# Transposes in a one-core encoder step: issued in groups, or one by one between the projections' matmuls

## The chip, the cores and the metric

The kernel runs on one core of a Trainium2 chip. The metric is device time in microseconds (us) of one execution. TensorE (PE, with its weight loads as PEld), VectorE (DVE), ScalarE (ACT), GpSimd (POOL) and the DMA queues of SyncE (SP) work side by side, each through its own list of instructions, and wait for one another by semaphores.

## What is computed

One inference step of a streaming encoder: two layers over 512 rows of a prompt and 8 x 16 rows of running streams, 640 rows in all, width 1024. The rows go through the same weights. Each layer adds a normalised mixer and then a normalised gated feed-forward block to its rows:

```python
for layer in range(DEPTH):
    hp = rms_norm(xp, norm_mix_pre[layer])
    hs = rms_norm(xs, norm_mix_pre[layer])
    if layer % 2 == 0:     # gated spatial mixing and a short convolution
        mp, _, hist_p = even_mixer(hp, zero_hist, *prm)
        ms, vn_s, hist_s = even_mixer(hs, cache_conv[e], *prm)
    else:                  # pooling over trailing windows, and attention
        mp, np_p, k_p, v_p = odd_mixer(hp, zero_pool, pos_p, *prm, None, None)
        ms, np_s, k_s, v_s = odd_mixer(hs, cache_pool[o], pos_s, *prm, cache_k[o], cache_v[o])
    xp = xp + rms_norm(mp, norm_mix_post[layer])
    xs = xs + rms_norm(ms, norm_mix_post[layer])
    fp = swiglu(rms_norm(xp, norm_ffn_pre[layer]), ffn_w_gate[layer], ffn_w_up[layer], ffn_w_down[layer])
    fs = swiglu(rms_norm(xs, norm_ffn_pre[layer]), ffn_w_gate[layer], ffn_w_up[layer], ffn_w_down[layer])
    xp = xp + rms_norm(fp, norm_ffn_post[layer])
    xs = xs + rms_norm(fs, norm_ffn_post[layer])
```

A mixer is `h @ w_in`, its two halves side by side, and `@ w_out`. The attention of the odd mixer has 8 heads of 64; a prompt row sees its own and earlier rows, a stream's 16 rows see 512 cached rows and each other.

## The kernel before

The 640 rows are five row tiles of 128, t = 0 to 3 of the prompt and t = 4 of the streams. The program runs the even mixer, a feed-forward block, the odd mixer and a second feed-forward block. Products are in fp32 accuracy: each operand is split into a high and a low part in the fast 32-bit format, on ScalarE (the cast, high) and on VectorE (the subtraction, low), and a product is three matmuls, high by high, high by low and low by high. Most of the mixers' and gates' products go through a seven-product scheme over halves of 320 rows (`Seven`, `GateUp`, with the operand tiles of `Quarters`): those are the matmuls with 320 columns. The value projections (`v_proj`) and output projections (`out_chunk`) have matmuls with 512 columns.

A matmul contracts over partitions, so a row tile must be turned first. `pre_norm` (L352) normalises a row tile into `xn`, issues eight 128x128 transposes of it on TensorE (`flip`, L169) into two PSUM banks, and then has the bank pair split by `take` (L317) into the operand tiles. The four normalisations make 160 transposes. In attention `prompt_stream` (L1083) turns the probabilities of two heads per item (80 transposes in 16 items), and `sample_stream` (L1151) turns five tiles of probabilities and then one of outputs per item (48 in 8 items). ScalarE copies the turned probabilities out of PSUM, and the products with the values follow.

What stands where on TensorE is decided twice. `Weave` (L48) runs generators: `main` (priority 9) issues the projections and yields every 6 to 15 matmuls; `pre_norm` (priority 0) and the attention streams (priority 1) go ahead of it when they are due. Due times are on an estimated clock, `W.now`, that every matmul and every transpose moves on. The framework's scheduler then sets the final order on each engine by its own estimates, with the instructions of `tc.high_priority()` first; in the first mixer ScalarE's and VectorE's first instructions stay in program order (`Ordered`, L87, its helper line is L99).

Line numbers of the profile: matmuls are L167, transposes L171, ScalarE's and VectorE's instructions L99, the reciprocal root on GpSimd L234.

Of the kernel before, what the change touches and what calls it, by code (L numbers as in the profile page):

```python
# [1 line left out]

# [12 lines left out]
P = 128  # L15
# [32 lines left out]
class Weave:  # L48
# [6 lines left out]
    def __init__(self):  # L55
        self.now = 0.0
        self.tasks = []
        self.made = 0

    def spawn(self, gen, prio=0, wait=0.0):  # L60
        self.made += 1
# [3 lines left out]
        event.at = self.now + wait  # L65

    def run(self):
        def due(t):
            return t[2].at if isinstance(t[2], Event) else t[2]

        while self.tasks:
            known = [t for t in self.tasks if due(t) is not None]
            assert known, "every task waits"
            ready = [t for t in known if due(t) <= self.now]
            if not ready:
                self.now = min(due(t) for t in known)
                continue
            t = min(ready, key=lambda t: t[:2])
            try:
                r = next(t[3])  # L80
            except StopIteration:
                self.tasks.remove(t)
                continue
            t[2] = r if isinstance(r, Event) else self.now + (r or 0.0)
# [21 lines left out]
def trunk_kernel(  # L106
# [57 lines left out]
    def mm(out, lhsT, rhs, start, stop, n, share=1, more=False):  # L164
        fast = lhsT.dtype == F32R
        W.now += PASS * (max(n, 256) if fast else 4 * n / share) + 2
        nc.tensor.matmul(out, lhsT=lhsT, rhs=rhs, start=start, stop=stop, skip_group_check=more)  # L167

    def flip(out, in_):  # L169
        W.now += 109  # L170
        nc.tensor.transpose(out=out, in_=in_, identity=ident)  # L171

    uid = [0]

# [4 lines left out]
    def bank(shape=(P, 512)):  # L179
        return psp.tile(list(shape), F32, tag="ps", name=nm("ps"))  # L180
# [171 lines left out]
    def pre_norm(t, x, X, wait, xn=None):  # L352
        if xn is None:
            xn = t4([P, D])
        with tc.high_priority():
            norm = Norm()
            norm.add(x, xn)
            r = norm.get()
            dve.scalar_tensor_tensor(out=xn, in0=x, scalar=r, in1=X.gain, op0=ALU.mult, op1=ALU.mult)
        yield wait  # L360
        ps = []
        for half in range(2):
            ps.append(bank((P, HK, P)))
            for i in range(HK):
                k = HK * half + i
                flip(ps[half][:, i, :], xn[:, k * P : (k + 1) * P])
        yield 500
        X.take(t, ps)

    class PostNorm:  # L370
# [562 lines left out]
    def odd_mixer(X):  # L933
# [149 lines left out]
        def prompt_stream(items):  # L1083


            for j, qt in items:
# [22 lines left out]
                for pr, sm in prs:  # L1109
                    ri = st()  # L1110
                    dve.reciprocal(out=ri, in_=sm)
                    dve.tensor_scalar(out=pr[:, :n], in0=pr[:, :n], scalar1=ri, scalar2=None, op0=ALU.mult)
                yield 2200 + 5 * n
                for h in range(2):
                    s, pr = ss[h], prs[h][0]
                    for kt in range(qt + 1):
                        flip(s[:, kt * P : (kt + 1) * P], pr[:, kt * P : (kt + 1) * P])
                    act.copy(out=pr[:, :n], in_=s[:, :n])
                yield 600 + 1.5 * n
                if j not in pos:  # L1120
                    pos[j] = bank()
                po = pos[j]
# [28 lines left out]
        def sample_stream(items):  # L1151
            for b in items:
# [31 lines left out]
                dve.tensor_tensor(out=ri, in0=sm[:, 0:1], in1=sm[:, 1:2], op=ALU.add)  # L1184
                dve.reciprocal(out=ri, in_=ri)
                yield 3300
                for kt in range(5):
                    flip(s[:, kt * P : (kt + 1) * P] if kt < 4 else s2[:, :P], pr[:, kt, :])
                pt = t2([P, 5, P])
                act.copy(out=pt[:, 0:4, :].rearrange("p a c -> p (a c)"), in_=s)  # L1190
                dve.tensor_copy(out=pt[:, 4, :], in_=s2[:, :P])
# [16 lines left out]
                os_ = pt[:, 0, :]  # L1208
                dve.tensor_scalar(out=os_, in0=o, scalar1=ri, scalar2=None, op0=ALU.mult)
                yield 500  # L1210
                flip(s2[:, 2 * P : 3 * P], os_)
                ot = s2[:, 2 * P : 3 * P].rearrange("p (a c s) -> p a c s", a=4, c=2)
                for h in range(2):
                    r = slice(64 * h, 64 * h + 64)
# [49 lines left out]
    def main():  # L1264
# [20 lines left out]
        next(first)  # L1285
        hls = [operand(w[0])]
        for _ in first:
            pass
        W.signal(X.top[0])
        hls.append(operand(w[1]))  # L1290
        start(1, A1)
# [118 lines left out]
```

## Time and profile before

| | us |
|---|---|
| median of three timed runs | 1320.55 (1320.53 to 1320.88) |
| the profiled execution | 1320.24 |
| its span | 1318.5 |
| TensorE busy | 1294.0 (98%) |
| VectorE busy | 889.0 (67%) |
| ScalarE busy | 614.0 (47%) |
| transposes, records of all 288 | 42.2 |

The span is the time from the profile's first to its last record. Busy shares are of that span. A record's length is the time from its issue to its modelled end, and records of neighbours overlap on TensorE, so the sum of records of a group is more than the time it takes on the array. Names of tiles in the rows are cut to their stem; `ps` is a PSUM bank, `q` the split of a weight, `x` and `a` splits of rows, `t` other tiles, `st` statistics.

### The profile page before, as it was taken

Reading aid. Unit: us, or ns where it says so; the run is one execution under the profiler, and the core shown is the slowest. Engines: PE = TensorE matmul, PEld = TensorE weight load, DVE = VectorE, ACT = ScalarE, POOL = GpSimd, SP = SyncE. Lnnn points to the kernel's source line nnn. Section 1 sums busy time; section 2 is a strip of 40 time slices with the busy share of each in tenths; the row PEclk is TensorE's granted clock in tenths of the full one; section 3 lists DMA queues with packets and bytes.
Section 4 is the critical chain, followed back from the end, with each engine's and each line's share of the span. In section 5 each row is a group of like instructions: output and inputs, shape, how many; then the busy total and the mean of one; then the engine's idle time right before and its main releaser. Section 6 shows DMA issues by size and latency. Waiting matters only on the chain.

```text
span 1318.5 us, 20069 instructions
## 1 busy us (share of the span) xinstructions
PE 1294.0 (98%) x8060; PEld 1178.4 (89%) x8060; DVE 889.0 (67%) x1452; ACT 614.0 (47%) x1130; POOL 54.9 (4%) x107
## 2 busy tenths in 40 slices
PE   6999999999999999999999999999999999999997
PEld 5998989989899998998799885789999898998996
DVE  6985779837576675776736556489557575864766
ACT  5644546535254352454433455366455261551551
POOL 2200101000000000000210000010000000000000
PEclk9999999999999999999999999999999999999999
DMA  7212253212223122126435336532213021230233
GB/s 249 73 65 81 96 200 138 96 48 81 96 73 120 53 77 112 64 84 218 163 120 195 147 143 250 197 128 102 107 64 128 32 98 63 96 115 30 97 128 128
DMA packets 45965, 150.12 MB, mean 114 GB/s; under 512 B 6576, under 2 KB 8496, under 8 KB 45872
## 3 DMA queue, kind: packets, MB, share of 16 engines
q1 hardware_dynamic: 45872, 148.84, 31.2%
q8 instruction: 63, 1.03, 0.3%
q14 instruction: 30, 0.25, 0.1%
HBM read 133.57 MB, written 15.26 MB: 113 GB/s over the span
## 4 chain that ended last, share of the span: by engine, by line
PE 86%; DVE 5%; issue 3%; ACT 2%; DMA 2%; POOL 1%; SPq 0%; DVEq 0%; POOLq 0%; ACTq 0%
PE ps L167 84%; DVE t L99 3%; PE ps L171 1%; DMA xbuf<-t 1%; POOL st L234 1%; ACT t L99 1%; DMA raw<-in_dram 1%; DVE q L99 1%; ACT q L99 1%; DVE x L99 1%; DVE st L99 0%; ACT ps L99 0%; ACT f L99 0%; POOL t L751 0%; SPq L380 0%
## 5 line engine op out<-in xcount | busy, mean ns | idle before, releaser
L167 PE MATMUL ps<-x,q 128*128 128x320 f32 (+2 forms) x4884 | 727.4, 309 | 1.2 <-DVE q L99 0.8
L167 PEld LDWEIGHTS ps<-x,q 128*128 128x128 f32 x4884 | 717.5, 188 | 6.2 <-issue 2.9
L167 PE MATMUL ps<-q,hid 128*128 128x512 f32 x1800 | 417.3, 391 | 0.2 <-DVE hid L99 0.2
L99 ACT CAST q<-raw 128x1024 fp32r<-128x1024 f32 (+1 forms) x278 | 269.7, 977 | 296.8 <-PE ps L167 247.1
L99 DVE TENSOR_TENSOR q<-raw,q 128x1024 fp32r<-128x1024 f32 (+1 forms) x278 | 313.9, 1132 | 134.4 <-ACT q L99 129.3
L167 PEld LDWEIGHTS ps<-q,hid 128*128 128x128 f32 x1800 | 335.5, 188 | 70.9 <-issue 1.7
L99 ACT COPY t<-ps 128x320 f32<-128x320 f32 (+2 forms) x304 | 135.0, 451 | 193.7 <-PE ps L167 173.8
L99 DVE TENSOR_TENSOR t<-ps,t 128x512 f32<-128x512 f32 (+2 forms) x164 | 100.3, 614 | 93.2 <-PE ps L167 93.0
L99 DVE TENSOR_TENSOR raw<-raw 128x512 f32<-128x512 f32 (+1 forms) x141 | 121.9, 866 | 11.6 <-DMA raw<-in_dram 10.0
L99 DVE TENSOR_TENSOR t<-t,t 128x512 f32<-128x512 f32 (+4 forms) x107 | 57.8, 551 | 48.5 <-ACT t L99 46.7
L234 POOL TENSOR_TENSOR st<-st,mhalf 128x1 f32<-128x1 f32 x45 | 31.7, 705 | 1005.9 <-DVE st L99 1001.1
L99 DVE SCALAR_TENSOR_TENSOR t<-t,st,t 128x512 f32<-128x512 f32 (+1 forms) x60 | 54.5, 925 | 16.6 <-POOL st L234 15.1
L99 ACT ACTIVATE t<-t 128x320 f32<-128x320 f32 (+1 forms) x60 | 40.1, 668 | 45.0 <-issue 26.2
L171 PE MATMUL ps<-ident,t 128*128 128x128 f32 x288 | 42.2, 281 | 12.0 <-DVE t L99 9.6
L171 PEld LDWEIGHTS ps<-ident,t 128*128 128x128 f32 x288 | 33.4, 143 | 21.9 <-DVE t L99 9.9
L99 ACT CAST hid<-t 128x320 fp32r<-128x320 f32 (+1 forms) x96 | 45.9, 482 | 11.1 <-DVE t L99 8.9
L99 DVE TENSOR_TENSOR t<-t 128x320 f32<-128x320 f32 (+3 forms) x90 | 48.8, 542 | 1.4
L99 DVE TENSOR_TENSOR hid<-t,hid 128x320 fp32r<-128x320 f32 (+1 forms) x96 | 48.8, 512 | 0.1
L167 PE MATMUL ps<-q,x 128*128 128x512 f32 x192 | 47.6, 402 | 1.2 <-DVE st L99 0.8
L99 ACT ACTIVATE ps<-t 128x512 f32<-128x512 f32 x40 | 24.1, 603 | 50.6 <-DVE t L99 50.6
L167 PEld LDWEIGHTS ps<-q,x 128*128 128x128 f32 x192 | 36.1, 192 | 10.6 <-DVE q L99 2.3
L99 DVE TENSOR_TENSOR t<-t,ps 128x320 f32<-128x320 f32 x47 | 22.9, 487 | 33.2 <-PE ps L167 33.2
(90 smaller groups left out, 497.5 us busy)
## 6 DMA issues: line engine op xcount, KB each, us to landing
raw<-in_dram SPq DMA_DIRECT2D x184, 512.0 KB, 4.1
x<-in_dram SPq DMA_DIRECT2D x24, 512.0 KB, 6.1
t<-in_dram SPq DMA_DIRECT2D x22, 512.0 KB, 5.8
xbuf<-t SPq DMA_DIRECT2D x15, 512.0 KB, 3.4
t<-xbuf SPq DMA_DIRECT2D x15, 512.0 KB, 3.9
out_dram<-t SPq DMA_DIRECT2D x15, 256.0 KB, 2.0
c<-in_dram SPq DMA_DIRECT2D x4, 512.0 KB, 4.2
fscr<-x SPq DMA_DIRECT2D x2, 768.0 KB, 3.3
```

Source lines behind the costliest of these rows:

```text
L99: ins = op(*args, **kw)
L167: nc.tensor.matmul(out, lhsT=lhsT, rhs=rhs, start=start, stop=stop, skip_group_check=more)
L171: nc.tensor.transpose(out=out, in_=in_, identity=ident)
L234: nc.gpsimd.tensor_tensor(out=r, in0=ms, in1=mhalf, op=ALU.pow)
```

## The change

Transposes are no longer issued where they are made. A generator that wants some hands a list to `flips`, which appends each to a queue and returns an event; the event is signalled when the last of that list has been issued. Every fast matmul takes one transpose off the queue behind itself, or two if it has more than 400 columns. When no generator is due the queue gives one. A transpose moves the estimated clock by 70 instead of 109. `pre_norm` takes both banks before its first transpose. In `prompt_stream` both heads' transposes are queued, each head's copy follows its own event, and the wait behind the copies is 600 + n instead of 600 + 1.5 n. The first row tile's transposes are drained at once in `main`.

```diff
@@ -1,3 +1,4 @@
+from collections import deque
 from contextlib import ExitStack
 
 import concourse.bass as bass
@@ -56,6 +57,14 @@
         self.now = 0.0
         self.tasks = []
         self.made = 0
+        self.flips = deque()
+    def flip_one(self):
+        issue, event, wait = self.flips.popleft()
+        issue()
+        if event is not None:
+            self.signal(event, wait)
 
     def spawn(self, gen, prio=0, wait=0.0):
         self.made += 1
@@ -65,13 +74,18 @@
         event.at = self.now + wait
 
     def run(self):
         def due(t):
             return t[2].at if isinstance(t[2], Event) else t[2]
 
         while self.tasks:
             known = [t for t in self.tasks if due(t) is not None]
-            assert known, "every task waits"
+            assert known or self.flips, "every task waits"
             ready = [t for t in known if due(t) <= self.now]
+            if not ready and self.flips:
+                self.flip_one()
+                continue
             if not ready:
                 self.now = min(due(t) for t in known)
                 continue
@@ -165,10 +179,21 @@
         fast = lhsT.dtype == F32R
         W.now += PASS * (max(n, 256) if fast else 4 * n / share) + 2
         nc.tensor.matmul(out, lhsT=lhsT, rhs=rhs, start=start, stop=stop, skip_group_check=more)
+        if fast:
+            for _ in range(min(len(W.flips), 2 if n > 400 else 1)):
+                W.flip_one()
 
     def flip(out, in_):
-        W.now += 109
+        W.now += 70
         nc.tensor.transpose(out=out, in_=in_, identity=ident)
+    def flips(pairs, wait=0.0):
+        event = Event()
+        for i, (out, in_) in enumerate(pairs):
+            last = event if i == len(pairs) - 1 else None
+            W.flips.append((lambda out=out, in_=in_: flip(out, in_), last, wait))
+        return event
 
     uid = [0]
 
@@ -358,13 +383,8 @@
             r = norm.get()
             dve.scalar_tensor_tensor(out=xn, in0=x, scalar=r, in1=X.gain, op0=ALU.mult, op1=ALU.mult)
         yield wait
-        ps = []
-        for half in range(2):
-            ps.append(bank((P, HK, P)))
-            for i in range(HK):
-                k = HK * half + i
-                flip(ps[half][:, i, :], xn[:, k * P : (k + 1) * P])
-        yield 500
+        ps = [bank((P, HK, P)) for _ in range(2)]
+        yield flips([(ps[k // HK][:, k % HK, :], xn[:, k * P : (k + 1) * P]) for k in range(NK)], 500)
         X.take(t, ps)
 
     class PostNorm:
@@ -1111,12 +1131,19 @@
                     dve.reciprocal(out=ri, in_=sm)
                     dve.tensor_scalar(out=pr[:, :n], in0=pr[:, :n], scalar1=ri, scalar2=None, op0=ALU.mult)
                 yield 2200 + 5 * n
+                turned = [
+                    flips(
+                        [
+                            (ss[h][:, kt * P : (kt + 1) * P], prs[h][0][:, kt * P : (kt + 1) * P])
+                            for kt in range(qt + 1)
+                        ]
+                    )
+                    for h in range(2)
+                ]
                 for h in range(2):
-                    s, pr = ss[h], prs[h][0]
-                    for kt in range(qt + 1):
-                        flip(s[:, kt * P : (kt + 1) * P], pr[:, kt * P : (kt + 1) * P])
-                    act.copy(out=pr[:, :n], in_=s[:, :n])
-                yield 600 + 1.5 * n
+                    yield turned[h]
+                    act.copy(out=prs[h][0][:, :n], in_=ss[h][:, :n])
+                yield 600 + n
                 if j not in pos:
                     pos[j] = bank()
                 po = pos[j]
@@ -1184,8 +1211,7 @@
                 dve.tensor_tensor(out=ri, in0=sm[:, 0:1], in1=sm[:, 1:2], op=ALU.add)
                 dve.reciprocal(out=ri, in_=ri)
                 yield 3300
-                for kt in range(5):
-                    flip(s[:, kt * P : (kt + 1) * P] if kt < 4 else s2[:, :P], pr[:, kt, :])
+                yield flips([(s[:, kt * P : (kt + 1) * P] if kt < 4 else s2[:, :P], pr[:, kt, :]) for kt in range(5)])
                 pt = t2([P, 5, P])
                 act.copy(out=pt[:, 0:4, :].rearrange("p a c -> p (a c)"), in_=s)
                 dve.tensor_copy(out=pt[:, 4, :], in_=s2[:, :P])
@@ -1208,7 +1234,7 @@
                 os_ = pt[:, 0, :]
                 dve.tensor_scalar(out=os_, in0=o, scalar1=ri, scalar2=None, op0=ALU.mult)
                 yield 500
-                flip(s2[:, 2 * P : 3 * P], os_)
+                yield flips([(s2[:, 2 * P : 3 * P], os_)])
                 ot = s2[:, 2 * P : 3 * P].rearrange("p (a c s) -> p a c s", a=4, c=2)
                 for h in range(2):
                     r = slice(64 * h, 64 * h + 64)
@@ -1285,7 +1311,8 @@
         next(first)
         hls = [operand(w[0])]
         for _ in first:
-            pass
+            while W.flips:
+                W.flip_one()
         W.signal(X.top[0])
         hls.append(operand(w[1]))
         start(1, A1)
```

Helper lines move: what was L99 is L113 in the changed kernel, L167 is L181 and L171 is L188. The orders of two engines in the first mixer and in attention show what moves.

TensorE in the value projection of the first mixer, before: `t_38` and `t_43` are the normalised row tiles 3 and 4, `ps_337` the product of row tile 2 (`q_92` the operand tile that holds it), `ps_425` that of row tile 3.

```order
L171 MATMUL ps_316<-ident,t_38_172 128x128 x4
L171 MATMUL ps_321<-ident,t_38_172 128x128 x4
L167 MATMUL ps_337<-q_124,q_92 128x512 x6
L167 MATMUL ps_337<-q_143,q_92 128x512 x6
L171 MATMUL ps_371<-ident,t_43_182 128x128 x4
L167 MATMUL ps_337<-q_154,q_92 128x512 x3
L171 MATMUL ps_376<-ident,t_43_182 128x128 x4
L167 MATMUL ps_337<-q_154,q_92 128x512 x3
L167 MATMUL ps_337<-q_157,q_92 128x512 x6
L167 MATMUL ps_425<-q_124,a_9_100 128x512 x2
```

The same place after; here row tile 2's product is `ps_329` and row tile 3's is `ps_396`.

```order
L181 MATMUL ps_329<-q_124,q_92 128x512
L181 MATMUL ps_329<-q_124,q_92 128x512
L188 MATMUL ps_317<-ident,t_38_172 128x128 x2
L181 MATMUL ps_329<-q_124,q_92 128x512 x2
L181 MATMUL ps_329<-q_143,q_92 128x512 x6
L181 MATMUL ps_329<-q_157,q_92 128x512 x6
L181 MATMUL ps_396<-q_124,a_9_100 128x512
L188 MATMUL ps_383<-ident,t_43_182 128x128 x2
L181 MATMUL ps_396<-q_124,a_9_100 128x512
L188 MATMUL ps_383<-ident,t_43_182 128x128 x2
L181 MATMUL ps_396<-q_124,a_10_101 128x512
L188 MATMUL ps_384<-ident,t_43_182 128x128 x2
```

Row tile 3's transposes have moved from ahead of tile 2's product into it, two behind each matmul, and row tile 4's from the middle of tile 2's product into tile 3's.

VectorE behind them, before: `q_528` is the low half of the weights of the first 320-column products, `x_99` a split of rows, `t_78` the last difference of row tile 3 and `t_82` the first of row tile 4.

```order
L99 BN_AGGR st_416<-st_414 128x2
L99 TENSOR_TENSOR q_528<-raw_525,q_528 128x1024
L99 TENSOR_TENSOR x_99<-t_78_358,x_99 128x4x128
L99 TENSOR_TENSOR t_82_399<-ps_376,t_81_397 128x512
L99 TENSOR_SCALAR st_418<-st_416 128x1
L99 TENSOR_TENSOR q_531<-raw_525,q_531 128x1024
L99 TENSOR_TENSOR t_83_400<-t_82_399,f_102 128x512
L99 TENSOR_TENSOR t_81_397<-f_102,t_81_397 128x512
L99 TENSOR_TENSOR x_96<-t_82_399,x_96 128x4x128
L99 TENSOR_TENSOR x_97<-t_83_400,x_97 128x4x128
L99 TENSOR_TENSOR x_98<-t_81_397,x_98 128x4x128
L99 TENSOR_TENSOR t_84_401<-t_83_400,f_103 128x512
```

After, where `t_88` is what `t_82` was, and `t_89`, `t_87`, `t_90` are the rest of row tile 4:

```order
L113 BN_STATS st_450<-ps_396 128x6
L113 TENSOR_TENSOR t_88_423<-ps_384,t_87_421 128x512
L113 TENSOR_TENSOR x_99<-t_78_358,x_99 128x4x128
L113 TENSOR_TENSOR t_89_424<-t_88_423,f_102 128x512
L113 TENSOR_TENSOR t_87_421<-f_102,t_87_421 128x512
L113 TENSOR_TENSOR x_96<-t_88_423,x_96 128x4x128
L113 TENSOR_TENSOR x_97<-t_89_424,x_97 128x4x128
L113 TENSOR_TENSOR x_98<-t_87_421,x_98 128x4x128
L113 TENSOR_TENSOR t_90_425<-t_89_424,f_103 128x512
L113 BN_AGGR st_452<-st_450 128x2
L113 TENSOR_TENSOR q_528<-raw_525,q_528 128x1024
L113 TENSOR_TENSOR x_99<-t_90_425,x_99 128x4x128
```

All of row tile 4's differences and splits but the last stand ahead of `q_528` now.

TensorE at the start of the 320-column products, before; `ps_536` and `ps_562` are the first two products.

```order
L167 MATMUL ps_536<-x_93,q_528 128x320 x12
L167 MATMUL ps_536<-x_94,q_528 128x320 x12
L167 MATMUL ps_562<-x_93,q_531 128x320 x12
L167 MATMUL ps_562<-x_94,q_531 128x320 x12
L167 MATMUL ps_588<-a_9_100,q_528 128x320
```

After:

```order
L181 MATMUL ps_536<-x_93,q_528 128x320 x2
L181 MATMUL ps_562<-x_93,q_531 128x320 x2
L181 MATMUL ps_588<-a_9_100,q_528 128x320
L181 MATMUL ps_588<-a_10_101,q_528 128x320
L181 MATMUL ps_614<-a_9_100,q_531 128x320
L181 MATMUL ps_614<-a_10_101,q_531 128x320
L181 MATMUL ps_666<-x_93,q_646 128x320 x2
L181 MATMUL ps_680<-x_94,q_646 128x320 x2
L181 MATMUL ps_536<-x_93,q_528 128x320 x10
L181 MATMUL ps_536<-x_94,q_528 128x320 x12
L181 MATMUL ps_562<-x_93,q_531 128x320 x10
```

Two matmuls each of six products stand ahead of the rest of the first one.

TensorE among the attention's samples, before: `ps_7827` and `ps_7828` are the two banks of one sample, `t_1084` its probabilities, `x_7822` its cached values, `t_1110` the copy of the turned probabilities; `t_805` is the query operand of another sample's scores.

```order
L171 MATMUL ps_7794<-ident,t_1091_7878 128x128
L171 MATMUL ps_7827<-ident,t_1084_7844 128x128 x3
L171 MATMUL ps_7828<-ident,t_1084_7844 128x128
L167 MATMUL ps_7828<-x_7822,t_1110_7996 32x128 x16
L167 MATMUL ps_7828<-x_5933,t_1110_7996 32x128 x4
L171 MATMUL ps_7932<-ident,t_1098_7949 128x128 x4
L171 MATMUL ps_7933<-ident,t_1098_7949 128x128
L171 MATMUL ps_7828<-ident,t_1110_7996 128x128
L167 MATMUL ps_7966<-x_7960,t_805_6440 32x512 x2
```

After, where a sample's banks are `ps_7893` and `ps_7894`, and `q_7332` a weight of the output projection:

```order
L181 MATMUL ps_7792<-q_7332,hid_6529 128x512
L188 MATMUL ps_7893<-ident,t_1094_7910 128x128
L181 MATMUL ps_7792<-q_7332,hid_6529 128x512
L188 MATMUL ps_7849<-ident,t_1097_7948 128x128
L188 MATMUL ps_7893<-ident,t_1094_7910 128x128 x2
L181 MATMUL ps_7792<-q_7332,hid_6529 128x512
L188 MATMUL ps_7893<-ident,t_1094_7910 128x128
L188 MATMUL ps_7894<-ident,t_1094_7910 128x128
L181 MATMUL ps_7894<-x_7888,t_1116_8052 32x128 x6
L181 MATMUL ps_8027<-x_8021,t_805_6440 32x512 x2
```

Matmuls of the output projection stand between the transposes of one sample; the products with the values, `ps_7894<-x_7888`, follow the last transpose as they did before.

## Rows read from the trace of the kernel before

**Rows 1.** The page: TensorE's busy time; its granted clock in 40 slices, tenths.

```profile
PE 1294.0 (98%) x8060; PEld 1178.4 (89%) x8060; DVE 889.0 (67%) x1452; ACT 614.0 (47%) x1130; POOL 54.9 (4%) x107
PEclk9999999999999999999999999999999999999999
```

**Rows 2.** TensorE's waits, whole run: engine, line, releaser: us in total, times, longest.

```profile
PE ps L171 <- DVE t L99: 9.6, 4, 8.0
```

**Rows 3.** The page's groups: line, engine, out<-in, count, busy us, mean ns, idle before.

```profile
L171 PE MATMUL ps<-ident,t 128*128 128x128 f32 x288 | 42.2, 281 | 12.0 <-DVE t L99 9.6
```

**Rows 4.** Timeline of TensorE, 186 to 226: start us, length us, instructions, idle before.

```profile
211.50 1.03 PE L171 MATMUL ps<-ident,t 128*128 128x128 f32 x8
...
214.14 3.78 PE L167 MATMUL ps<-x,q 128*128 128x320 f32 x24 [0.43 <-DVE q L99]
...
220.58 1.03 PE L171 MATMUL ps<-ident,t 128*128 128x128 f32 x8
221.37 4.64 PE L167 MATMUL ps<-x,q 128*128 128x320 f32 x30
225.85 0.46 PE L167 MATMUL ps<-a,q 128*128 128x320 f32 x2
```

**Rows 5.** Timeline of TensorE in the odd mixer, 723.7 to 725.5.

```profile
724.63 0.38 PE L171 MATMUL ps<-ident,t 128*128 128x128 f32 x2
724.76 0.42 PE L167 MATMUL ps<-x,q 128*128 128x384 f32 x1
725.02 0.38 PE L171 MATMUL ps<-ident,t 128*128 128x128 f32 x2
```

**Rows 6.** Timelines of TensorE and its weight loads around 840.

```profile
840.11 0.71 PE L167 MATMUL ps<-q,hid 128*128 128x512 f32 x2
...
840.63 0.14 PEld L171 LDWEIGHTS ps<-ident,t 128*128 128x128 f32 x1 [0.25 <-DVE t L99]
...
840.72 6.63 PE L167 MATMUL ps<-q,hid 128*128 128x512 f32 x28
```

**Rows 7.** Timeline of TensorE in the first mixer, 30 to 62.

```profile
32.31 0.66 PE L171 MATMUL ps<-ident,t 128*128 128x128 f32 x4 [0.38 <-ACT vn L99]
...
43.05 2.88 PE L167 MATMUL ps<-q,x 128*128 128x512 f32 x12
45.77 7.20 PE L167 MATMUL ps<-x,q 128*128 128x320 f32 x48
52.81 1.92 PE L167 MATMUL ps<-a,q 128*128 128x320 f32 x12
```

**Rows 8.** Timeline of VectorE in the first mixer, 32.5 to 50.

```profile
38.54 0.69 DVE L99 BATCH_NORM_STATS2 st<-ps 128x6 f32<-128x512 f32 x1
...
42.84 1.19 DVE L99 TENSOR_TENSOR q<-raw,q 128x1024 fp32r<-128x1024 f32 x1
43.98 0.69 DVE L99 TENSOR_TENSOR x<-t,x 128x512 fp32r<-128x512 f32 x1
...
45.19 0.14 DVE L99 TENSOR_SCALAR st<-st 128x1 f32<-128x1 f32 x1
...
46.38 0.69 DVE L99 TENSOR_TENSOR t<-t,f 128x512 f32<-128x512 f32 x1
...
49.99 0.15 DVE L99 SCALAR_TENSOR_TENSOR st<-st,st 128x1 f32<-128x1 f32 x1
```

**Rows 9.** Timeline of VectorE at the first feed-forward block, 206 to 222.

```profile
216.19 0.42 DVE L99 TENSOR_TENSOR t<-f,t 128x256 f32<-128x256 f32 x1
...
218.91 1.28 DVE L99 SCALAR_TENSOR_TENSOR t<-t,st,t 128x1024 f32<-128x1024 f32 x1 [0.44 <-POOL st L234]
```

**Rows 10.** Attention: TensorE's waits from 720 to 845, then timeline of TensorE there.

```profile
PE ps L167 <- ACT t L99: 1.9, 2, 1.4
PE ps L167 <- DMA x<-in_dram: 0.7, 1, 0.7
...
829.01 1.30 PE L167 MATMUL ps<-x,t 128*32 128x128 f32 x40 [1.38 <-ACT t L99]
```

## The prediction

> **What bounds the kernel now.** I began with the page's busy times and its clock row: TensorE is busy for 1294.0 of the 1318.5 us of the span, and the granted clock stands at its top level, 2.4 GHz, in every slice [rows 1]. So the time is TensorE's list of instructions plus the little that it waits, and the clock has nothing to give back. The second view was TensorE's waits over the whole run: the largest sum, 9.6 us in front of transposes, holds one wait of 8.0 us for the first row tile, which the change leaves alone [rows 2]. The rest of those is 1.6 us, and the two sums in attention that the change can reach are 1.9 and 0.7 us [rows 10]. A gain from filled waits can thus be a few us at most, 0.2 or 0.3%.
>
> The third view was the cost of a transpose. The mean of 281 ns on the page is the length of a record, which overlaps its neighbours [rows 3]; the pitch is what counts. In the first products after the value projection 48 matmuls of 320 columns take 52.81 - 45.77 = 7.04 us, 0.147 each, and ahead of them 12 of 512 columns 45.77 - 43.05 = 2.72, 0.227 each [rows 7]. From the eight transposes at 220.58 to 225.85 there are 5.27 us, in which 30 such matmuls also lie [rows 4]: 5.27 - 30 x 0.147 = 0.86, or 0.108 for a transpose. (I measure over the whole stretch because the record of the matmul behind a transpose starts before the array is free for it.) All 288 cost about 31 us, 2.4% of the span.
>
> **The change part by part.** *The same work, spread.* Counted in the two orders of TensorE, 25 transposes stood alone, 16 in pairs and 247 in threes and fours; now 109 stand alone, 128 in pairs and 51 in threes and fours. No matmul and no transpose comes or goes. So the question is what a lone one costs. The nearest case is in the odd mixer, where one matmul of 384 columns stands between two pairs: from pair to pair it is 725.02 - 724.63 = 0.39 us [rows 5]. The matmul takes 0.147 x 384/320 = 0.176, and 0.214 is left, 0.107 for each of the two. The first of that pair has a matmul ahead of it and the second one behind it, as a lone one has both, and together they cost what two in a group of eight do. Spreading by itself gains nothing and loses little. From above the price is bounded by a lone transpose late in attention: two 512-column matmuls start at 840.11 and the next run at 840.72. At 0.227 each the two take 0.454, so 0.156 lies between, 0.048 over a grouped one, and there the transpose's own weight load had waited 0.25 for VectorE [rows 6]. Between 0 and 0.048 I take 0.006, near rows 5, because most others won't have waited: 109 x 0.006 = 0.65 us.
>
> *Other work that moves.* A transpose counts less on the planner's clock, and the queue empties only as matmuls go by, so what follows the transposes comes at another time. TensorE's two orders differ in five places and are the same elsewhere.
>
> Place A, the first mixer, 26 to 62 us. Tile 4's transposes now stand among the products of tile 3 instead of tile 2, and on VectorE all of tile 4's splits now stand ahead of the low half of q_528, the weights of the first feature products. In the trace that low half runs from 42.84 to 43.98 [rows 8]. Now these stand ahead of it as well: the last split of tile 3 and the first difference of tile 4 (43.98 to 45.19, 1.21), a statistics step (a record of 0.69 with 0.09 of overlap, 0.60) and the rest of tile 4 (46.38 to 49.99, 3.61): 5.42 us, on an engine without idle time in this stretch. So it starts at 48.26 and is released near 49.45. TensorE reached its first 320-column product at 45.77; its wait of 0.38 for the second bank falls away [rows 7], so it comes there at 45.39. Two matmuls each of six products now stand at its head, those that need only high halves: 12 x 0.147 = 1.76, to 47.15. The next is the third of the first product, which needs the low half: TensorE stands for 2.3 us. Before, the same twelve matmuls' worth was done at 45.77 + 1.76 = 47.53, so the loss is 49.45 - 47.53 = 1.9, taken as **2.0** with the pass of the semaphore; 1.4 to 2.6, as VectorE runs some tenths earlier or later. Nothing behind it gives this back, because TensorE hardly waits for the next 100 us.
>
> Places B and E, the starts of the two feed-forward blocks' first products (186 to 226, and 860 to 900 in layer 2). Tile 4's transposes stand 11 matmuls earlier, 11 x 0.147 = 1.62, so TensorE gets there at 220.58 - 1.62 = 218.96 [rows 4]; the normalised tile was ready at 218.91 + 1.28 = 220.19 [rows 9]. VectorE's new order has that step ahead of three small steps, of which one record is 0.42 with 0.08 of overlap [rows 9]: about 1.0 earlier, 219.2. A wait of about 0.25 is left. The old wait of 0.43 for q [rows 4] may go or stay. I take +0.25 for each place, from -0.5 (that wait goes and no new one comes) to +1.0 (the step keeps most of its old time).
>
> Place C, the start of the odd mixer, 616 to 662: the 1.6 us of waits of rows 2 that lie outside the start can shrink, while splits of weights come later, as in A. No row prices it; I take 0, with 0.6 either way.
>
> Place D, attention, 720 to 845. Here TensorE's products waited 1.9 us in two waits for a copy of the probabilities and 0.7 for a DMA; the row at 829.01 shows the pattern, 40 small products that waited 1.38 for the copy behind five transposes [rows 10]. Projection matmuls now fill some of these. But a transposes' run now ends later, by the matmuls in it, and at three points in the new order the small products stand right behind their tile's last transpose, with no matmul that covers the copy. By 829.01, where part was covered, the three cost 0.4 to 1.4 each. Taken away up to 2.6, added about 2.6: I take 0, from -3 to +2.
>
> The sum: 2.0 + 2 x 0.25 + 0 + 0 + 0.65 = 3.15 us. The profiled execution took 1320.24 (its span and 1.74 around it); with the sum 1323.4. The median of the timed runs, 1320.55, stands 0.31 above it, so I forecast **1323.7**.
>
> The pair of rows 5 costs 0.214, although the weight load of its first transpose had a long matmul to hide under. The Trainium skill, "TensorE: Matmul & The Clock Gate", section "Step-by-step: what each phase is for", says that the next weights load while the running matmul streams, and section "Back-to-back issue gap" gives about 81 ns for a load and a 128-column matmul in a stream; by that figure, an estimate, 109 lone ones would give back 109 x 0.027 = 2.9 us and the sum would end near 1320.8. The trace does not agree: the price in rows 4 and 5 is 107 to 108 ns.
>
> **The rivals.** *Not slower:* the matmuls between attention's transposes do cover the copies. Place: the samples in 790 to 845. Price: D's 3.0, so 1320.7. It decides from where some 6 matmuls of 512 columns (1.38/0.227) stand between a tile's last transpose and its small products. For it: the waits are there [rows 10]. Against: three such places have none, and A's stall, which it must pay for, is worked out from rows. 27%.
>
> *Faster:* a lone transpose costs less than a grouped one, its load being hidden. The bounds are nothing and 0.108; at half, 109 x 0.054 = 5.9 less than the forecast: 1317.8. Against it stand rows 5; it needs the matmul behind a transpose not to be what sets the price. 6%.
>
> *Slower, lone ones dear:* each costs the 0.048 of rows 6 instead of 0.006, 109 x 0.042 = 4.6 more: 1328.3. Against it: the one in that row had waited. 4%.
>
> *Slower in B and E:* the normalised tiles are not earlier, and TensorE stands a full 1.2 us (220.19 - 218.96) ahead of each of the four sets of transposes that moved up: 4 x 1.2 instead of 0.5, so 1328.0. It decides by whether VectorE's step ends before 219.5. 5%.
>
> **How the numbers follow.** The forecast, A's stall with D within 1.5 us of nothing, has 58%. 0.2% is 2.64 us, about what a measurement of this kernel can tell from no change: faster is under 1317.9, slower over 1323.2. The forecast lies close above that border, so of its 58% I count 38 as slower and 20 as the same. Slower: 0.38 + 0.04 + 0.05 = 0.47. Same: 0.20 and 0.25 of the first rival, 0.45. Faster: 0.06 and the last 0.02 of the first rival, 0.08. The range takes in D's ends and the first rival, 1319.4 to 1327.4, and leaves out the faster rival and the two slower ones.
>
> **What would show it.** Right: the low half of q_528 on VectorE near 48.3, a TensorE wait of 2 to 3 us for it that ends near 49.5, a pitch of lone transposes still near 0.108, and short waits of transposes near 212 and 219. Wrong: no wait at 47 us, so that A's 2.0 falls out; a lone pitch under 0.09; or the stretch of attention shorter or longer by over 2 us.

## The result, and the profile after

The changed kernel takes 1326.50 us (median of 6, 1325.14 to 1327.19) where the kernel before takes 1320.76 (6 runs, 1320.53 to 1320.91). The ratio is 1.0042 with a 95% interval of 1.0029 to 1.0055: slower, by 5.7 us. The forecast was 1323.7 with a range of 1319.4 to 1327.4. So the direction is right and the time lies in the range, but the loss is nearly twice the 3.15 us of the sum. The profiled execution of the changed kernel took 1327.19, the slowest of the six, with a span of 1325.5. What follows is read from that trace, in which the loss is 7.0 us and not 5.7.

TensorE's busy time and its waits after, as on the page and in the view of its waits (answering to [rows 1, 2]):

```profile
PE 1296.4 (98%) x8060; PEld 1179.3 (89%) x8060; DVE 888.8 (67%) x1452; ACT 616.7 (47%) x1130; POOL 57.2 (4%) x107
...
PE ps L188 <- DVE t L113: 11.9, 7, 8.0
PE ps L181 <- DVE q L113: 4.2, 3, 2.4
PE ps L188 <- DVE st L113: 2.6, 3, 1.2
PE ps L181 <- ACT t L113: 2.1, 3, 0.9
```

Before, the row for the split of a weight (`q`) was

```profile
PE ps L167 <- DVE q L99: 1.0, 3, 0.4
```

These waits have thus gone from 1.0 (three, the longest 0.4) to 4.2 us, those of transposes for a row tile on VectorE (`t`) from 9.6 to 11.9. The largest new one is 2.4 us. Here it is on TensorE's timeline (start, length, instructions, idle time ahead), and VectorE's timeline at the same place (answering to [rows 7, 8]):

```profile
46.31 0.75 PE L181 MATMUL ps<-x,q 128*128 128x320 f32 x4
49.47 8.25 PE L181 MATMUL ps<-x,q 128*128 128x320 f32 x44 [2.41 <-DVE q L113]
57.56 1.63 PE L181 MATMUL ps<-a,q 128*128 128x320 f32 x10
...
48.23 1.18 DVE L113 TENSOR_TENSOR q<-raw,q 128x1024 fp32r<-128x1024 f32 x1
```

The low half of q_528 begins at 48.23 (forecast 48.26) and TensorE goes on at 49.47 (forecast 49.45). But the row behind the wait holds something that the forecast had not: 44 matmuls take 57.56 - 49.47 = 8.09 us, 0.184 each, where the same matmuls took 0.147 before [rows 7]. The view by stretches (us, then the busy time and count of PE, PEld, DVE, ACT and POOL, the granted clock, the DMA share, GB/s) says why:

```profile
49.00:50.00 1.00, 0.53 (x3) 0.53 (x4) 1.00 (x3) 0.00 (x0) 0.00 (x0) 1.00 0.00 0
50.00:51.00 1.00, 1.00 (x7) 1.00 (x6) 1.00 (x3) 0.00 (x0) 0.78 (x1) 0.60 0.00 0
51.00:52.00 1.00, 1.00 (x6) 1.00 (x5) 0.55 (x3) 0.14 (x1) 0.63 (x1) 0.50 0.00 0
52.00:53.00 1.00, 1.00 (x5) 1.00 (x5) 1.00 (x2) 0.63 (x1) 0.00 (x0) 0.50 0.62 172
53.00:54.00 1.00, 1.00 (x6) 1.00 (x6) 1.00 (x3) 0.00 (x0) 0.00 (x0) 0.69 1.03 401
54.00:55.00 1.00, 1.00 (x9) 1.00 (x8) 1.00 (x3) 0.00 (x0) 0.57 (x1) 1.00 1.07 430
```

The granted clock falls to 0.50, 1.2 of 2.4 GHz, less than 1 us after TensorE has resumed from its wait, and is back some 3.4 us later. TensorE works through them without a pause, but at half speed. By the four rows the lost work is 0.40 + 0.50 + 0.50 + 0.31 = 1.7 us. The page cannot show it: a slice of it is 33 us long, and its digit for the clock is a 9 throughout, as before.

Where the 7 us went was found by counting TensorE's records back from the end in both traces, since the two lists are as long and the same outside the five places. The difference in time of the same matmul, from stretch to stretch, in us (one trace of each kernel, borders by the times of before):

| stretch | forecast | after minus before |
|---|---|---|
| A, to 160 | +2.0 | +3.66 |
| between, 160 to 186 | 0 | +0.34 |
| B, to 226 | +0.25 | +0.70 |
| C, to 662 | 0 | +2.07 |
| D, attention, 720 to 860 | 0 | -2.17 |
| E, to 900 | +0.25 | +1.38 |
| behind E, to 940 | 0 | +0.96 |
| borders of transposes | +0.65 | in the places |
| sum | +3.15 | +6.94 |

Attention did gain, and every other place lost more than I had put there.

### The profile page after: what moved, and what is told of

It reads as the page before. It is cut to its first block, busy times and chain, and to the rows that moved or that the text cites. A ratio compares the mean times of both kernels' runs of the same rounds, so it can differ in the third digit from the quotient of the medians.

```text
span 1325.5 us, 20079 instructions
## 1 busy us (share of the span) xinstructions
PE 1296.4 (98%) x8060; PEld 1179.3 (89%) x8060; DVE 888.8 (67%) x1452; ACT 616.7 (47%) x1130; POOL 57.2 (4%) x107
## 5 line engine op out<-in xcount | busy, mean ns | idle before, releaser
L181 PE MATMUL ps<-x,q 128*128 128x320 f32 (+2 forms) x4884 | 735.0, 311 | 3.1 <-DVE q L113 2.4
L181 PEld LDWEIGHTS ps<-x,q 128*128 128x128 f32 x4884 | 722.4, 188 | 8.5 <-issue 2.9
L181 PE MATMUL ps<-q,hid 128*128 128x512 f32 x1800 | 430.2, 394 | 0.8 <-ACT t L113 0.4
L113 DVE TENSOR_TENSOR q<-raw,q 128x1024 fp32r<-128x1024 f32 (+1 forms) x278 | 313.9, 1132 | 141.4 <-ACT q L113 135.0
L113 ACT CAST q<-raw 128x1024 fp32r<-128x1024 f32 (+1 forms) x278 | 269.7, 977 | 297.6 <-PE ps L181 250.3
L181 PEld LDWEIGHTS ps<-q,hid 128*128 128x128 f32 x1800 | 334.8, 188 | 71.6 <-issue 2.6
L113 ACT COPY t<-ps 128x320 f32<-128x320 f32 (+3 forms) x304 | 135.3, 451 | 195.9 <-PE ps L181 181.4
L113 DVE TENSOR_TENSOR t<-ps,t 128x512 f32<-128x512 f32 (+2 forms) x164 | 100.3, 614 | 91.0 <-PE ps L181 90.5
L113 DVE TENSOR_TENSOR raw<-raw 128x512 f32<-128x512 f32 (+1 forms) x141 | 121.8, 866 | 13.4 <-DMA raw<-in_dram 11.4
L113 DVE TENSOR_TENSOR t<-t,t 128x512 f32<-128x512 f32 (+4 forms) x107 | 57.9, 550 | 48.6 <-ACT t L113 46.3
L188 PE MATMUL ps<-ident,t 128*128 128x128 f32 x288 | 58.8, 278 | 14.5 <-DVE t L113 11.9
L113 DVE SCALAR_TENSOR_TENSOR t<-t,st,t 128x512 f32<-128x512 f32 (+1 forms) x60 | 54.4, 926 | 17.6 <-POOL st L259 16.2
L188 PEld LDWEIGHTS ps<-ident,t 128*128 128x128 f32 x288 | 38.9, 143 | 24.5 <-DVE t L113 9.5
L113 ACT ACTIVATE t<-t 128x320 f32<-128x320 f32 (+1 forms) x60 | 40.1, 668 | 39.9 <-DVE t L113 20.8
L113 ACT CAST hid<-t 128x320 fp32r<-128x320 f32 (+1 forms) x96 | 45.9, 482 | 12.3 <-DVE t L113 10.1
L181 PE MATMUL ps<-q,x 128*128 128x512 f32 x192 | 48.7, 405 | 2.7 <-DVE q L113 1.8
L113 DVE TENSOR_TENSOR t<-t 128x320 f32<-128x320 f32 (+3 forms) x90 | 48.7, 541 | 1.4
L113 DVE TENSOR_TENSOR hid<-t,hid 128x320 fp32r<-128x320 f32 (+1 forms) x96 | 48.8, 512 | 0.1
L181 PEld LDWEIGHTS ps<-q,x 128*128 128x128 f32 x192 | 36.1, 192 | 12.5 <-DVE q L113 4.2
L113 DVE TENSOR_TENSOR t<-t,ps 128x320 f32<-128x320 f32 x47 | 22.9, 487 | 32.5 <-PE ps L181 32.5
L113 ACT ACTIVATE ps<-t 128x512 f32<-128x512 f32 x40 | 24.0, 600 | 41.4 <-DVE t L113 41.4
```

The lines of the kernel that those rows point to most:

```text
L113: ins = op(*args, **kw)
```

## The experiments

The theory at the start: the loss in the first mixer comes from the number 70 on the planner's clock (by the orders of VectorE, in which q_528 stands late with 70 whether transposes are spread or not), and spreading itself is harmless; the gain in attention is real. The rival: spreading the normalisations' transposes is what delays VectorE and costs the time.

**One number alone.**

```diff
--- before
+++ e1_cost_only
     def flip(out, in_):
-        W.now += 109
+        W.now += 70
```

> The kernel before with one number changed: a transpose moves the planner's clock by 70 instead of 109; transposes stay in groups. On VectorE the low half of q_528 then stands behind the splits of row tile 4, as in the changed kernel. Theory (the loss in the first mixer comes from the number, not from the spreading): TensorE waits 2 to 2.5 us for that low half near 47 us, and the clock falls behind it, so place A costs 3 to 4 us and the time is 1323.5 to 1325. Rival (spreading delays VectorE): no wait at 47 us, 1320.8 within 0.7.

Measured: 1327.93 us, ratio 1.0054 (1.0041 to 1.0067). Not one transpose is spread, and the kernel loses at least as much as the changed one (the two intervals overlap). TensorE's timeline in the first mixer has the same wait as after:

```profile
49.33 6.92 PE L167 MATMUL ps<-x,q 128*128 128x320 f32 x35 [2.45 <-DVE q L99]
```

It was expected at 1323.5 to 1325; place A came out at +3.46 as expected, but B and what lies ahead of it lost 1.98 and attention 2.83, of which 2.04 is a wait for a transfer (before, 0.7 [rows 10]):

```profile
830.33 1.10 PE L167 MATMUL ps<-x,t 128*32 128x512 f32 x12 [2.04 <-DMA x<-in_dram]
```

with the clock at 0.50 behind it once more, from about 831.4 to 834.8. The profiled execution took 1329.85, 1.9 above the median of its kernel, so not every execution paid all of this. Place A has the wait without one spread transpose, which speaks for the number there and against the rival; the next run tries the other side.

**Spreading alone.**

```diff
--- after
+++ e2_spread_109
     def flip(out, in_):
-        W.now += 70
+        W.now += 109
...
-                yield 600 + n
+                yield 600 + 1.5 * n
```

> The changed kernel with the two estimates put back (109 a transpose, 600 + 1.5 n behind the copies); transposes are queued and issued one by one as in the changed kernel. Theory: no wait for q_528 in the first mixer, so 3.7 us come back and the time is near 1322.8 (1321.5 to 1324), the waits of row tiles 3 and 4 in the feed-forward blocks' starts (0.8 each) still there. Rival (spreading costs it): 1326.5 within 1.

Measured: 1322.97 us, ratio 1.0015 (1.0007 to 1.0024). That is the forecast time, but not by the forecast way alone: A's loss is nearly gone (+0.32 instead of +3.66), so there the number is the cause. Attention gains 4.37 instead of 2.17. The waits of 0.8 for row tiles in the feed-forward blocks' starts, which were expected to stay, are gone, and B and E each have a longer one for the low half of a weight, in B with the lower clock behind it:

```profile
216.66 5.03 PE L181 MATMUL ps<-x,q 128*128 128x320 f32 x22 [2.34 <-DVE q L113]
...
218.00:219.00 1.00, 1.00 (x6) 1.00 (x5) 1.00 (x2) 0.98 (x2) 0.00 (x0) 0.50 1.15 356
219.00:220.00 1.00, 1.00 (x5) 1.00 (x5) 1.00 (x5) 0.82 (x2) 0.00 (x0) 0.50 0.83 303
220.00:221.00 1.00, 1.00 (x5) 1.00 (x5) 1.00 (x3) 0.56 (x2) 0.00 (x0) 0.50 0.76 311
...
891.19 3.50 PE L181 MATMUL ps<-x,q 128*128 128x320 f32 x22 [2.33 <-DVE q L113]
```

These two runs make a square with the kernels before and after: groups at 109 take 1320.8, groups at 70 1327.9, spread at 109 1323.0, spread at 70 1326.5. The number costs 7.1 us in groups and 3.5 spread. Spreading, attention and normalisations together, costs 2.2 at 109 (the interval of e2 lies clear of 1); at 70 the difference of 1.4 is within the intervals. (The wait behind attention's copies is 600 + n in the last of the four alone.)

**Half of the change each.**

```diff
--- after
+++ e3_attention_only
     def pre_norm(t, x, X, wait, xn=None):
...
-        ps = [bank((P, HK, P)) for _ in range(2)]
-        yield flips([(ps[k // HK][:, k % HK, :], xn[:, k * P : (k + 1) * P]) for k in range(NK)], 500)
+        ps = []
+        for half in range(2):
+            ps.append(bank((P, HK, P)))
+            for i in range(HK):
+                k = HK * half + i
+                flip(ps[half][:, i, :], xn[:, k * P : (k + 1) * P])
+                W.now += 39
+        yield 500
```

> Only attention's transposes are queued; those of the four normalisations stay in groups, at 109 each. TensorE's order differs from before in attention alone. Theory (in attention the change gains 2.2 us, all loss is in the normalisations): 1318.6 (1318.0 to 1319.4), TensorE's waits for the copies of probabilities smaller than before. Rival (the gain there was only time that earlier stalls had given to the transfers): 1320.8 within 0.5.

The other half, `e4_norm_only`, queues in `pre_norm` and has the two attention streams issue theirs at once, with `W.now += 39` behind each and the wait of 600 + 1.5 n.

> Only the normalisations' transposes are queued, with 70 each; attention's stay in groups at 109. Theory: all of the loss without the gain in attention, 1328.7 (1327.5 to 1330). Rival (attention's part of the change does nothing): 1326.5 within 1.

Measured: attention alone 1319.10 us, ratio 0.9985 (0.9977 to 0.9994), a gain; the normalisations alone 1327.65, ratio 1.0049 (1.0035 to 1.0062). In the first, TensorE passes attention in 1.86 us less than before and stands within 0.5 of before in every other stretch. In the second, attention gives nothing (+0.05) and the first mixer costs 4.36, with the wait of 2.56 ahead of 50.21 in place of 2.41. Both as expected by the theory.

**The wait taken away.** The changed kernel, with only the place of one split on VectorE moved:

```diff
--- after
+++ e5_no_stall
-            self.cols = [unit(feed) for _ in range(2)]
+            if isinstance(self, PlainUnits):
+                raw0 = next(feed)
+                with tc.high_priority():
+                    self.cols = [operand(raw0)]
+                self.cols.append(unit(feed))
+            else:
+                self.cols = [unit(feed) for _ in range(2)]
```

> The changed kernel, with the first pair of weights in the first mixer split at high priority, so that the low half of q_528 stands ahead of row tile 4's splits on VectorE; the transposes and the planner's numbers as in the changed kernel. Theory (place A costs 3.7: 2.0 net of standing and 1.6 of the lower clock behind it): no wait near 47 us, the granted clock 1.00 from 49 to 55, and 1326.5 - 3.7 = 1322.8 (1322 to 1323.6). Rival (the clock's fall has another cause, as that the spread transposes leave TensorE less busy): only the 2.0 come back, 1324.5, with the clock at 0.50 for some us in 45 to 60.

Measured: 1322.49 us (ratio to before 1.0013, 1.0004 to 1.0022), 4.0 less than after. TensorE's timeline has no wait there, and 48 matmuls take 52.99 - 45.95 = 7.04 us as before; the stretch behind is at full clock:

```profile
45.95 7.20 PE L181 MATMUL ps<-x,q 128*128 128x320 f32 x48
52.99 1.92 PE L181 MATMUL ps<-a,q 128*128 128x320 f32 x12
...
50.00:54.00 4.00, 4.00 (x29) 4.00 (x28) 3.55 (x9) 1.56 (x4) 0.87 (x1) 1.00 0.18 67
```

The transposes are spread as in the changed kernel, so the lower clock came from the wait and not from the spreading.

**A longer wait, in the kernel before.** Here VectorE writes the same low half three times, the last time behind the splits of row tile 4:

```diff
--- before
+++ e6_longer_stall
-            self.cols = [unit(feed) for _ in range(2)]
+            raw0 = next(feed)
+            q = operand(raw0)
+            if isinstance(self, PlainUnits):
+                for _ in range(2):
+                    dve.tensor_tensor(out=q[:, 1, :], in0=raw0, in1=q[:, 0, :].bitcast(F32), op=ALU.subtract)
+            self.cols = [q, unit(feed)]
```

> The kernel before, with transposes in groups, in which VectorE writes the low half of q_528 three times over (the same values). The last one ends near 51.8 (42.84 and 8.95 us of work in its new order), TensorE comes at 47.5 and stands for 4.3 us. Theory (a stall of over 2 us is followed by some 3 us at half clock, however long it is, which costs 1.6): 4.3 + 1.6 = 5.9 more, 1326.7. Rival (no lower clock without spread transposes): 4.3 more, 1325.1. Rival (the time at the lower clock grows with the stall): over 7 more, 1328 or above.

Measured: 1327.12 us (ratio 1.0049, 1.0036 to 1.0063), 6.5 more than the 1320.63 of before beside it, and +6.00 in the first mixer by the trace:

```profile
46.86 0.46 PE L167 MATMUL ps<-x,q 128*128 128x320 f32 x2
51.37 8.72 PE L167 MATMUL ps<-x,q 128*128 128x320 f32 x46 [4.06 <-ACT vn L99]
...
52.00:53.00 1.00, 1.00 (x6) 1.00 (x7) 1.00 (x3) 0.00 (x0) 0.00 (x0) 0.71 0.00 0
53.00:54.00 1.00, 1.00 (x6) 1.00 (x5) 1.00 (x3) 0.00 (x0) 0.20 (x1) 0.50 0.00 0
54.00:55.00 1.00, 1.00 (x5) 1.00 (x5) 0.79 (x1) 0.00 (x0) 1.00 (x1) 0.50 0.47 98
55.00:56.00 1.00, 1.00 (x6) 1.00 (x6) 0.77 (x3) 0.57 (x1) 0.20 (x1) 0.59 0.85 328
```

(This wait was ended by ScalarE's `vn`, as the row says, and not by the weight: VectorE's last write of it began at 50.59 and took 1.20, to 51.79, when TensorE had already gone on. `vn` began at 50.55, as early as before (50.64), so it is TensorE's new order, and not a later `vn`, that made it wait there. The stall has the length that was wanted, by another way than was expected.) The wait is 4.06 us, the lost work behind it by the clock's rows 0.29 + 0.50 + 0.50 + 0.41 = 1.7 us, as much as behind the 2.41 of after. The price of the clock did not grow with the wait, and it is paid with transposes in groups too.

**Attention alone, with the old numbers.**

```diff
--- e3_attention_only
+++ e7_attention_109
     def flip(out, in_):
-        W.now += 70
+        W.now += 109
...
-                W.now += 39
...
-                yield 600 + n
+                yield 600 + 1.5 * n
```

> Only attention's transposes are queued, and the two estimates are those of before (109, and 600 + 1.5 n). Theory (the number 70, not the spreading, is what hurts the order, in attention too): attention gains 4.4 us, as in the trace of the kernel that spreads all at 109, so 1316.5 to 1317.5. Rival (the number does nothing in attention): 1319.1, as with 70.

Measured: 1317.09 us, ratio 0.9971 (0.9960 to 0.9981). Two numbers were put back together here, and which of them does it was not tried. The profiled execution was 1319.97, the slowest of the eight: attention gained 1.92 in it, and 1.31 were lost ahead of 160. The kernel was therefore run again:

> The same kernel as e7 once more, for a second trace, since the profiled execution of e7 took 1319.97 where its median is 1317.09 and its trace does not show the gain. Theory (the gain lies in attention's own stretch): TensorE passes 720 to 860 in 4 us less than before, 1316.5 to 1317.5 in all. Rival (the gain comes from elsewhere, attention gives the 1.9 us of e7's trace): a stretch of 1.5 to 2.5 less, and the rest of the gain at another place.

Measured: 1316.83 us, ratio 0.9970 (0.9959 to 0.9982), and in this profile, an execution of 1316.63, attention takes 4.00 us less and no other stretch differs by more than 0.2. TensorE's waits from 720 to 866 are two now, against the four before, 3.4 us in all, of which [rows 10] show the first two:

```profile
PE ps L181 <- ACT t L113: 0.4, 1, 0.4
PE ps L188 <- DVE t L113: 0.4, 1, 0.4
```

This kernel beats both: 3.9 us faster than before and 9.7 faster than the changed one.

Its two traces have the same order and differ by 2.1 us in attention. In the slower one, 0.8 of this lies at a wait for a transfer that the other does not have,

```profile
840.20 1.10 PE L181 MATMUL ps<-x,t 128*32 128x512 f32 x12 [0.58 <-DMA x<-in_dram]
```

and 1.3 in the small products just ahead of it; what held those up is not shown. So a stretch of attention in one trace is good to some 2 us only. That 109 does better there than 70 rests on the medians (1317.09 and 1316.83 against 1319.10).

Set against the kernel that spreads all at 109, this one also prices the other half at the old number: spreading the normalisations' transposes as well takes 1322.97 instead of 1316.83, some 6 us more, of which by the traces 2.8 lie in 160 to 226 and 2.9 in 860 to 940. So spreading is not harmless, as the theory at the start had it. In place A the number delays the weight; at the starts of the feed-forward blocks the rival holds, since with the old number TensorE waits 2.34 and 2.33 there for the low half of a weight on VectorE, and with the normalisations in groups no wait for one is longer than 0.5.

All kernels, by TensorE's matched records against before, in us:

| kernel | to 160 | 160 to 226 | 600 to 662 | 720 to 860 | 860 to 940 | all |
|---|---|---|---|---|---|---|
| after | +3.66 | +1.04 | +2.07 | -2.17 | +2.34 | +6.94 |
| e1, 70 in groups | +3.46 | +1.98 | -0.49 | +2.83 | +1.82 | +9.60 |
| e2, spread at 109 | +0.32 | +2.97 | +0.65 | -4.37 | +2.91 | +2.47 |
| e3, attention at 70 | -0.11 | +0.14 | +0.18 | -1.86 | +0.49 | -1.16 |
| e4, normalisations at 70 | +4.36 | +0.94 | +2.35 | +0.05 | +0.93 | +8.63 |
| e5, no wait in A | +0.18 | +0.89 | +2.17 | -2.15 | +1.39 | +2.48 |
| e6, longer wait | +6.00 | +0.14 | +0.37 | +0.09 | -0.01 | +6.60 |
| e7, attention at 109 | +1.31 | -0.01 | +0.19 | -1.92 | +0.13 | -0.29 |
| e8, the same again | 0.00 | +0.20 | +0.19 | -4.00 | -0.01 | -3.62 |

## Why the prediction came out as it did

*What bounds the kernel:* right, TensorE's list and its waits. The half sentence that the clock "has nothing to give back" was true and led past the other side: it has something to lose.

*The price of a lone transpose:* right. In the changed kernel's trace (TensorE's timeline in place B) lone ones stand between 320-column matmuls at a pitch of 215.74 - 215.48 = 0.26 us:

```profile
215.48 0.27 PE L188 MATMUL ps<-ident,t 128*128 128x128 f32 x1
215.51 0.40 PE L181 MATMUL ps<-x,q 128*128 128x320 f32 x1
215.74 0.27 PE L188 MATMUL ps<-ident,t 128*128 128x128 f32 x1
```

Less the matmul's 0.147 this is 0.113 against 0.108 in a group: 0.005 more, where 0.006 was taken (24 such pitches in this trace lie between 0.257 and 0.264). The number of them was too high: by TensorE's records 89 transposes stand between two matmuls, against 7 before, so 82 became lone and not 109, which also counts those that stand beside a transpose into another bank. Both rivals on this price fall, and so does the sum that was worked out from the 81 ns of the Trainium skill, "TensorE: Matmul & The Clock Gate", section "Back-to-back issue gap"; no row here comes near that figure for these fp32 transposes. (That sum had kept the 0.65 for dearer lone ones, which it replaces; without it the estimate would have ended near 1320.2.)

*Place A:* the order and the moment at which TensorE goes on are right to 0.03 us, the standing time to 0.1 (2.41 for 2.3), and its loss too: the matmuls that were done at 47.53 before would be done at 49.47, 1.94 later. The term was mis-sized by the clock behind it, some 1.7 us (3.66 in all). The prediction costed a wait at its length alone. e5 gives both back at once and e6 shows the same second part behind a wait made on purpose. As to the cause of the new order, the prediction named the planner's clock and the queue together; e1 and e2 show that in A it is the number alone.

*Places B and E:* too low, +0.70 and +1.38 for +0.25 each. The step that failed is "about 1.0 earlier" for the normalised tile. TensorE waited for it:

```profile
223.60 0.30 PE L188 MATMUL ps<-ident,t 128*128 128x128 f32 x1 [0.79 <-DVE t L113]
...
222.17 1.28 DVE L113 SCALAR_TENSOR_TENSOR t<-t,st,t 128x1024 f32<-128x1024 f32 x1 [0.44 <-POOL st L259]
```

The step stands earlier in VectorE's list, but it still had to wait 0.44 for the root from GpSimd, as before [rows 9]. With the lateness of 3.72 that this part of the trace has (200 us), it began at 222.17 - 3.72 = 218.45 against 218.91: 0.46 earlier and not 1.0. Moving an instruction ahead in a list gains no more than its input gains. By the prediction's own test, whether the step ends before 219.5, the rival *slower in B and E* (5%) holds: it ended at 218.45 + 1.28 = 219.73. TensorE stood 0.8 us ahead of each of the four sets of transposes, where that rival had 1.2 and the forecast about 0.25.

*Behind E:* +0.96 that the prediction did not have. At 925.62 TensorE waited 0.69 for a copy on ScalarE. Ahead of this wait ScalarE and VectorE are some 7 us behind before and TensorE 5.98, so TensorE catches up on them there. VectorE's waits from 845 to 928 show a releaser that they did not have before, the transposes, and TensorE's timeline shows when these came (the first and the last of row tile 4):

```profile
DVE x L113 <- PE ps L188: 1.3, 2, 1.0
...
900.15 0.30 PE L188 MATMUL ps<-ident,t 128*128 128x128 f32 x1 [0.79 <-DVE t L113]
...
902.00 0.27 PE L188 MATMUL ps<-ident,t 128*128 128x128 f32 x1
...
925.62 4.66 PE L181 MATMUL ps<-x,q 128*128 128x320 f32 x30 [0.69 <-ACT t L113]
```

With eight transposes among eight matmuls the last starts 1.85 us behind the first, where a group of eight takes 0.86 in all [rows 4]. That VectorE's lateness follows from this is argued from these rows and was not tried by itself.

*Place C:* wrong, +2.07 where 0 with 0.6 either way stood. The words "splits of weights come later, as in A" named what happened, and then no price was put on it:

```profile
648.19 1.66 PE L181 MATMUL ps<-q,x 128*128 128x512 f32 x6 [1.48 <-DVE q L113]
650.62 1.06 PE L188 MATMUL ps<-ident,t 128*128 128x128 f32 x8 [0.76 <-DVE st L113]
```

VectorE's list could have been added up there as it was in A. It appears in the kernels that have both 70 and spread normalisations (after, e4, e5: +2.07 to +2.35) and hardly in e1 or e2 (-0.49, +0.65); how the two work together there was not tried.

*Place D:* inside its bounds, -2.17 for 0, but outside the 1.5 us either way that the forecast's chance rested on, and by the prediction's own signs (attention over 2 us shorter) just wrong. The mechanism of the first rival, filled waits, is there; two waits for copies are left, 1.4 us together (the longer 0.94), where 2.6 were added for three bare places. At 109 the gain is 4.0 in one trace, more than the 3.4 us of waits in the stretch before, of which 0.8 stay. What the rest of it is stays open.

*The sum:* 3.15 against 6.94 in the trace and 5.74 in the medians. The direction was reasoned: A carried most of it (without A, in e5, 1.9 us of loss are left). That the time stayed in the range is in part luck: the surplus of C, E and the clock, for which the range had hardly any room, was partly paid for by attention's gain. Without that gain, as in e4, the time is 1327.65, above the range's end of 1327.4.

## What to carry to other kernels

Cost a long wait of TensorE (here from 2.0 us) at its length plus what the clock can take behind it (here 1.7 us), and look for that in a view of 1 us stretches, since a page of long slices does not show it. Before a change to an order is judged, separate what it does to the work from what it does to the planner's estimates: here one number moved unrelated splits on another engine and cost 7.1 us by itself, about as much as spreading the normalisations' transposes at the old number (some 6). Take the part that gains where TensorE has waits to fill (attention, 3.9 us) and leave it off where TensorE then waits for a split on VectorE (the normalisations, in e2).

## What was not expected of the hardware

Seven waits of TensorE of 2.0 us or more behind the kernel's start stand in these traces (2.04, 2.33, 2.34, 2.41, 2.45, 2.56 and 4.06), and behind six of them the granted clock fell to 0.50 within 1.4 us of TensorE's resuming, for some 3.4 us in which TensorE was fully busy. By the 1 us stretches the lost work was 1.7 us each time, behind the shortest of the six (2.04) as behind the longest (4.06). Behind the seventh (2.33 us, in e2 at 891) it stayed at 1.00. Behind none of the waits from 0.9 to 1.54 us did it fall. What tells the seventh from the others is open. Each kernel's traces show one execution (the last kernel's two); whether the clock fell in the others too is not shown. The six times of the changed kernel lie 2.05 us apart, those of before 0.38.
